# New prices in the clock model that sets a hybrid kernel's issue order: TensorE's spacings and the port of VectorE and GpSimd

## The chip, the core and the metric

The kernel runs on one core of a Trainium2 chip. Five engines take part: TensorE (PE, with its weight loads as PEld), VectorE (DVE), ScalarE (ACT), GpSimd (POOL) and SyncE (SP), which issues the transfers. The metric is the device time of one execution in microseconds (us). Before the change it is 1357.74 us, the median of three runs.

## What is computed

The reference is a backbone of two layers over 1024 latent tokens and a prefix of 256 context tokens, 1024 columns wide, all in float32. Cut to what matters, one layer is:

```python
shift, scale, gate = split(silu(c) @ w_mod + b_mod, 3)            # the context has its own
h = rms_norm(x) * (1 + scale) + shift
p = h @ w_in                                                     # one projection for all branches
a = silu(layer_norm(depthwise_conv31(p.a_val * sigmoid(p.a_glu)))) * silu(p.a_gate)
b = windowed_attention(rope(p.b_q), rope(p.b_k), p.b_v,          # 8 heads, 2 kv heads, +-128 tokens,
                       context keys and values, sink) * silu(p.b_gate)   # and all of the context
g = gla(p.c_q, p.c_k, p.c_v, decay(p.c_lr), chunk=64)            # forwards plus backwards, 4 heads
x = x + gate * (concat(a, b, norm(g) * silu(p.c_gate)) @ w_out)
```

At the end the latent tokens get a last RMSNorm. In the backward and the forward GLA each chunk of 64 tokens adds `(k * exp(b_last - b)).T @ v` to a state that decays from chunk to chunk; `b` is the running sum of the logarithms of the decay.

## The kernel before

The whole problem stays in SBUF as far as it can. Token tiles have 128 rows: two of context (0 and 1) and eight latent ones (2 to 9). Every large product is done in three float32r passes (`three`, L670): high part by high part, high by low and low by high, on weights that `piece` (L615) loads by DMA and splits into two parts (`split`, L362: a copy on ACT or DVE and a subtraction on DVE or POOL). Outputs of 256 or 512 columns accumulate in PSUM banks. A layer runs in two phases. `phase_a` (L1568) makes the projections, the convolution, the GLA and the attention's operands; `phase_bc` (L1627) runs attention and the out-projection side by side.

The pieces of the work that the change touches through the order:

- `conv_taps` (L921): 62 operations on DVE a layer (31 taps by two halves of the channels), `scalar_tensor_tensor` of 1295 columns in layer 0 and 1024 in layer 1, both inputs in SBUF. One is put in whenever DVE has no more than 300 ns of work in the model.
- `rope` (L883), called by `ev_qk_b` (L895) for each pair of token tiles: for each tile of the pair four `tensor_tensor` on POOL (a product with the sine, one with the cosine, a subtraction, an addition), eight a pair. The columns are 128 for the keys and 256 for the queries.
- `gla_states` (L1056), once for each direction `d` (forwards 0, backwards 1) and each of three chunks of columns `c` (256 context tokens, 512 and 512 latent ones): DVE subtracts (`last - b`), ACT takes the exponential, POOL multiplies by the keys in `mix`, PE transposes the product 128 columns at a time (`idr`), ACT copies the result from PSUM, PE makes the state products with the values in four column groups (outputs 32x128), and DVE adds them up chunk by chunk (`scalar_tensor_tensor` on 128x64).
- `u_run` (L1300), `u_head` (L1356), `u_ev` (L1375) and `u_pv` (L1384): a unit of attention is one block of 128 queries and one kv head. PE makes the scores of four heads, DVE the mask and the minimum, ACT the exponential with its sum, then the probabilities are scaled on DVE, POOL or ACT (`scale`, L383). PE transposes them, key tile by key tile and for four heads at a time, ACT and DVE write the high and the low part of each transposed tile (`H`), and PE multiplies them by the values (PV).
- `out_tiles` and `out_mm` (L1465, L1442): the out-projection, at low priority, which fills PE's time between attention's steps.

The order is not written out by hand. Every piece of work is a generator, a lane; what it yields is the condition for its next stage. `loop` (L201) keeps a clock `now`, which is PE's clock in the model, and issues among the stages whose conditions hold by then the one of the highest priority; if there is none, it goes on to the earliest. The conditions are times out of `Model`: `issue` (L117) starts each instruction when its engine and its operands are free, adds the price that `cost` (L94) gives, and notes on the parts of the tiles when they were written and read. `pick` (L356) chooses the engine for work that several can do: the one that would end first by these clocks. `Model` only decides order and engine. What has to wait for what on the chip is up to the semaphores, so a price that is off gives an order that suits the chip less, and nothing else: each engine takes its instructions strictly in the order of issue. Every instruction is issued through `Engine` (L35), so that the profile shows L43 for all of them (L44 after the change).

The model knows one more thing of PE: after an idle time of over 3 us it doubles the prices for 3.8 us (`cold`). It knew nothing of DVE and POOL hindering each other.

Of the kernel before, what the change touches and what calls it, by code (L numbers as in the profile page):

```python
# [34 lines left out]
class Engine:  # L35
    """an engine whose instructions are also put on the model's clock"""
# [12 lines left out]
class Model:  # L49
    """Estimate of when each engine is free and when each part of a tile was last written and read.  # L50
    It only decides the order in which instructions are issued; what has to wait for what is up to Tile."""

    def __init__(self, nc):
        self.nc = nc
        self.clock = dict(pe=0.0, act=0.0, dve=0.0, pool=0.0, sp=0.0, ring=0.0, dma=0.0)
        self.mem, self.memo = {}, {}
        self.end = self.cold = 0.0
        for n, a in (("pe", "tensor"), ("act", "scalar"), ("dve", "vector"), ("pool", "gpsimd"), ("sp", "sync")):
            setattr(self, a, Engine(self, n, getattr(nc, a)))

    def part(self, ap):
        """the times of ap's tile (written, read, written as seen by PE) and the pieces of it that ap covers"""
# [31 lines left out]
    def cost(self, e, op, out, ins, accum=0):  # L94
        n = out.free_size()
        if e == "pe":
            n = ins[-1].free_size()
            p = out.partition_size()
            if ins[0].dtype == F32R:
                return 55.0 if op == "transpose" else max(n / 2.4, 0.84 * p)  # L100
            return (1 if op == "transpose" else 2) * max(n / 1.2, 0.84 * p)
# [13 lines left out]
        return 110 + 1.1 * n  # L115

    def issue(self, e, op, a, k):  # L117
# [19 lines left out]
        else:  # L137
            x = self.cost(e, op, out, ins, len(outs) - 1)
            if e == "pe":
                if "tile_position" in k:  # L140
                    x = x * out.partition_size() / 128.0 + 29
# [15 lines left out]
class Lane:  # L157
    """a generator of stages: what it yields says when its next stage may be issued"""
# [6 lines left out]
class Hybrid:  # L165
# [10 lines left out]
    # ---------------------------------------------------------------- issue order  # L176
# [6 lines left out]
    def when(self, c, lane):  # L183
        """the time from which condition c holds, None if that is not known yet"""
# [16 lines left out]
    def loop(self, last):  # L201
        """issues stages until lane `last` is done: of those that may start by now, the first by priority"""
# [33 lines left out]
    # ---------------------------------------------------------------- memory  # L236
    def memory(self):
# [13 lines left out]
        # a PSUM tile is used by one engine at a time, so there is one a bank, but for two of two banks  # L251
# [18 lines left out]
    def choice(self, cls, wide):  # L270
        """the free slots; those for wide tiles are left to these while self.rsv"""
# [18 lines left out]
    def mix_new(self, dt):  # L290
        """the upper half of mix anew, to hold what it doesn't hold yet"""
# [6 lines left out]
    def mix(self, a, t, p=slice(None)):  # L298
        """tokens t of mix a, or of several that lie in the same half of mix"""
# [6 lines left out]
    def bank_of(self, cls, pair):  # L306
        """the bank that class cls would get"""
# [35 lines left out]
    def at(self, ap):  # L343
        """condition: all that has been issued has written ap"""
        return lambda: self.nc.written(ap)

    def rest(self, ap):
        """condition: nothing issued uses ap any more"""
        return lambda: self.nc.touched(ap)

    def sm_spare(self, cols):
        """like sm(), from the spare place if that is free"""
        return self.get("SF")[:, 0:cols] if self.slots["SF"] else self.sm(cols)

    # engines that can do the same work: the one that is done first
    def pick(self, *opts):  # L356
        """opts: (engine, estimated cost, function)"""
# [4 lines left out]
    def split(self, hi, lo, src):  # L362
        """hi + lo = src exactly, both float32r; src in SBUF"""
# [6 lines left out]
    def copy(self, o, a):  # L370
        """from PSUM"""
# [11 lines left out]
    def scale(self, o, a, s, f=1.0):  # L383
        """o = a * s * f; s one value a partition"""
# [6 lines left out]
    def square(self, junk, a, o):  # L391
        """o = sum of a * a"""
# [6 lines left out]
    # ---------------------------------------------------------------- set-up  # L399
# [37 lines left out]
    def rope_free(self):  # L437
        """between its uses the memory of the rotary table is one more small tile"""
# [3 lines left out]
    def rope_load(self):  # L442
        """generator: the rotary table again"""
# [24 lines left out]
    # ---------------------------------------------------------------- modulation  # L468
    def mod_add(self, l, b0, mt):
        """blocks b0 .. of the modulation from PSUM [128, blocks, 2], with their bias"""  # L470
# [9 lines left out]
    def mod_group(self, l, b0, n, raw):  # L480
        """generator: n blocks of 128 columns of the modulation, four k-tiles at a time in the column groups of the PE array;
        raw: the k-tiles of w_mod, loaded here if None"""
# [32 lines left out]
    # ---------------------------------------------------------------- h  # L515
    def hslot(self, i):
        """chunk and column offset of token tile i in the T-layout h"""
# [6 lines left out]
    def views(self):  # L524
        """the memory of h, free for it once the first weights have gone through"""
# [14 lines left out]
    def rstd(self, ss, scale, n):  # L540
        """(ss * scale + eps) ** -0.5 on [128, n]"""
# [13 lines left out]
    def part_h(self, l, i, k0, n, x):  # L555
        """generator: k-tiles k0 .. k0 + n - 1 of h for token tile i, from its normalised [128, 128 n] piece x"""
# [36 lines left out]
    def first_x(self, i, xt):  # L593
        """generator: token tile i of the input, loaded to xt and normalised there"""
# [16 lines left out]
    # ---------------------------------------------------------------- weights  # L611
# [14 lines left out]
    def load_w(self, key, src, ap, tile=None):  # L626
        """256 weight columns, split into hi and lo; ap(hl, k): k-tiles k and k + 1"""
# [22 lines left out]
    def loader(self):  # L650
        """generator: all weights in the order of their use"""
# [17 lines left out]
    # ---------------------------------------------------------------- in-projection  # L669
    def three(self, out, st, mv, k0, k1):  # L670
        """out += st(hi,lo)^T mv(hi,lo) over k-tiles k0 .. k1 - 1 of 8, three float32r passes"""
# [1159 lines left out]
```

## Time and profile before

| | |
|---|---|
| median of three runs | 1357.74 us (1356.18, 1357.74, 1364.62) |
| span of the profiled execution | 1357.4 us, 24183 instructions |
| mean granted clock of PE | 0.983 |
| busiest engines | PE 1268.0, PEld 1084.6, DVE 951.0, ACT 558.6, POOL 543.8 us |
| idle of PE, 0 to 200 us (loads, modulation, first projections) | 21.6 us |
| idle of PE, 1300 to 1357 us (tail of the out-projection) | 8.7 us |

The profiled execution is one run; its span is compared with sums made from its own rows, and the median with other medians. A row of the profile has the operation, output and inputs by the program's tile names, partitions by elements, type and count. The names: `ps` is a PSUM bank, `WS` split weights, `WR` raw weights and temporaries, `H` and `HC` the split activations and, later, attention's operands, `SM` small tiles, `mix` the branch outputs and the convolution's accumulators, `U` the convolution's input, `idr` the identity matrix. In brackets behind a row of the timeline stands how long the engine had been idle and who released it. A float32 matmul counts as two in the count of a row. "Clock" is the TensorE clock that was granted, 1.0 being full speed.

### The profile page before, as it was taken

What the parts mean: (1) busy time and instruction counts of PE and PEld (TensorE: products, weight loads), DVE (VectorE), ACT (ScalarE), POOL (GpSimd) and SP (SyncE); (2) the same over time, 40 slices, a digit from 0 to 9 for tenths busy, and PEclk for the clock granted to TensorE, in tenths of its full rate; (3) what the DMA queues carried; (4) which work ended last, traced back from release to release, by engine and by line L of the source; (5) the groups of instructions that cost most, each with busy time, mean ns of one, the idle gap of its engine ahead of it and who ended that gap; (6) DMA issues with size and microseconds to landing.
All of it is one profiled execution on the core that took longest, in us unless ns stands there. A gap on an engine that the chain in (4) does not pass through costs nothing.

```text
span 1357.4 us, 24183 instructions
## 1 busy us (share of the span) xinstructions
PE 1268.0 (93%) x9070; PEld 1084.6 (80%) x9070; DVE 951.0 (70%) x1852; ACT 558.6 (41%) x1239; POOL 543.8 (40%) x769
## 2 busy tenths in 40 slices
PE   6999986898999999999999989988899999999997
PEld 3667976787788676887998978977797888898997
DVE  5844895789655366875666686896957478887864
ACT  3720351121223364665663451251113156776751
POOL 1410046766222233464353032046783244645530
PEclk9999997899999999999999999989999999999999
DMA  9353112321212433343113452113322113311112
GB/s 331 137 147 97 55 32 58 83 79 44 67 32 65 131 118 89 104 129 97 42 55 98 132 191 62 55 37 78 97 57 77 34 48 101 98 44 51 62 37 78
DMA packets 105045, 116.46 MB, mean 86 GB/s; under 512 B 38464, under 2 KB 65376, under 8 KB 104928
## 3 DMA queue, kind: packets, MB, share of 16 engines
q1 hardware_dynamic: 104928, 114.92, 28.4%
q8 instruction: 71, 1.16, 0.3%
q14 instruction: 46, 0.38, 0.1%
HBM read 95.47 MB, written 19.42 MB: 85 GB/s over the span
## 4 chain that ended last, share of the span: by engine, by line
PE 49%; DVE 10%; POOL 8%; issue 5%; DMA 4%; ACT 2%; SPq 0%; POOLq 0%; DVEq 0%; ACTq 0%
PE ps L43 49%; DVE SM L43 5%; POOL SM L43 5%; DVE H L43 2%; DMA WR<-in_w_in_dram 2%; POOL WR L43 2%; DVE WS L43 1%; DVE mix L43 1%; ACT SM L43 1%; POOL tir L43 1%; DMA SM<-kd 0%; DMA SM<-x 0%; SPq L43 0%; DMA WR<-in_w_out_dram 0%; DMA x<-SM 0%
## 5 line engine op out<-in xcount | busy, mean ns | idle before, releaser
L43 PE MATMUL ps<-H,WS 128*128 128x512 f32 x1344 | 339.2, 400 | 4.2 <-DVE stat L43 2.4
L43 PEld LDWEIGHTS ps<-H,WS 128*128 128x128 f32 x1344 | 245.6, 189 | 71.4 <-issue 17.6
L43 ACT ACTIVATE SM<-ps 128x512 f32<-128x512 f32 (+4 forms) x172 | 91.0, 533 | 427.0 <-PE ps L43 353.5
L43 PE MATMUL ps<-WS,H 128*128 128x256 f32 x1704 | 254.0, 291 | 6.3 <-DVE SM L43 3.7
L43 PEld LDWEIGHTS ps<-WS,H 128*128 128x128 f32 x1704 | 229.2, 195 | 21.9 <-issue 11.6
L43 PE MATMUL ps<-idr,SM 128*128 128x128 f32 (+1 forms) x1076 | 150.1, 272 | 34.6 <-POOL SM L43 27.8
L43 DVE SCALAR_TENSOR_TENSOR mix<-U,small,mix 128x1295 f32<-128x1295 f32 (+1 forms) x120 | 176.6, 1517 | 0.2
L43 PEld LDWEIGHTS ps<-idr,SM 128*128 128x128 f32 (+1 forms) x1076 | 122.8, 142 | 58.3 <-POOL SM L43 32.9
L43 DVE SCALAR_TENSOR_TENSOR H<-ps,H 128x512 fp32r<-128x512 f32 x160 | 106.2, 683 | 59.7 <-ACT H L43 59.6
L43 POOL TENSOR_TENSOR SM<-SM,SM 128x256 f32<-128x256 f32 (+4 forms) x89 | 70.5, 799 | 179.8 <-ACT SM L43 142.6
L43 ACT ACTIVATE H<-ps 128x512 fp32r<-128x512 f32 x176 | 99.6, 597 | 86.7 <-PE ps L43 81.6
L43 POOL TENSOR_TENSOR tir<-tir,mhalf 128x1 f32<-128x1 f32 (+2 forms) x55 | 44.4, 810 | 205.3 <-DVE tir L43 177.8
L43 ACT ACTIVATE SM<-SM,stat 128x641 f32<-128x641 f32 (+2 forms) x144 | 110.4, 768 | 34.9 <-DVE stat L43 27.1
L43 DVE CUSTOM_DVE_ANT_0 SM<-ps,SM,small 128x640 f32<-128x640 f32 (+2 forms) x128 | 101.9, 808 | 18.8 <-PE ps L43 18.5
L43 PE MATMUL ps<-H 128*128 128x512 f32 x320 | 99.3, 412 | 2.0 <-DVE H L43 1.8
L43 PE MATMUL ps<-H,H 128*128 128x256 f32 x552 | 98.2, 286 | 0.0
L43 POOL TENSOR_TENSOR SM<-SM,WR 128x128 f32<-128x128 f32 (+2 forms) x113 | 88.5, 801 | 13.1 <-DVE SM L43 9.3
L43 PE MATMUL ps<-SM,SM 128*32 128x128 f32 (+4 forms) x764 | 80.3, 291 | 13.4 <-DVE SM L43 8.8
L43 POOL TENSOR_SCALAR SM<-SM,tir 128x640 f32<-128x640 f32 (+2 forms) x86 | 73.5, 869 | 38.5 <-DVE tir L43 30.4
L43 PEld LDWEIGHTS ps<-H,H 128*128 128x128 f32 x552 | 82.3, 189 | 4.7 <-issue 3.4
L43 PE MATMUL ps<-WS,SM 128*128 128x256 f32 x248 | 69.4, 280 | 0.0
L43 PE MATMUL ps<-H,SM 128*128 128x256 f32 x248 | 69.4, 280 | 0.0
(150 smaller groups left out, 2126.7 us busy)
## 6 DMA issues: line engine op xcount, KB each, us to landing
WR<-in_w_in_dram SPq DMA_DIRECT2D x80, 256.0 KB, 3.9
WR<-in_w_mod_dram SPq DMA_DIRECT2D x64, 256.0 KB, 3.0
WR<-in_w_out_dram SPq DMA_DIRECT2D x32, 256.0 KB, 3.3
SM<-vd SPq DMA_DIRECT2D x116, 64.0 KB, 2.4
x<-SM SPq DMA_DIRECT2D x20, 256.0 KB, 2.5
SM<-x SPq DMA_DIRECT2D x20, 256.0 KB, 4.6
qd<-SM SPq DMA_DIRECT2D x18, 256.0 KB, 2.2
mix<-in_x_dram SPq DMA_DIRECT2D x8, 512.0 KB, 8.0
```

The lines of the kernel that those rows point to most:

```text
L43: r = getattr(self._e, op)(*a, **k)
```

## The change

No instruction of the computation is changed. Three prices of the model are, and the order and the choice of engines follow from them:

1. `cost`, for PE. A float32r matmul of n columns costs max(64, n / 2.4 + 14) ns instead of max(n / 2.4, 0.84 p) with p output partitions; a float32r transpose max(64, n / 2.4) instead of 55. A float32 matmul costs 2 max(58, n / 1.2 + 5) instead of 2 max(n / 1.2, 0.84 p), and a float32 transpose 109 instead of max(n / 1.2, 0.84 p).
2. `issue`, for matmuls in column groups (`tile_position`): the price scaled by the partitions plus 29 ns gets a lower bound, half the full price for more than 64 columns and the full price otherwise.
3. `shared`, new. The model keeps the last 64 intervals of DVE instructions that have two SBUF inputs, or are a `tensor_copy` or `tensor_scalar` wholly in SBUF, and of POOL instructions that read SBUF. An instruction of that kind whose start falls into an interval of the other engine starts at its end. Its own price stays the same. The prices of ACT, DVE and POOL, the lanes, their priorities and all conditions stay the same too.

Comments and docstrings are removed besides, which shifts line numbers by one or more.

```diff
@@ class Model: __init__
         self.mem, self.memo = {}, {}
+        self.port = dict(dve=deque(maxlen=64), pool=deque(maxlen=64))
         self.end = self.cold = 0.0
@@ cost
             n = ins[-1].free_size()
-            p = out.partition_size()
             if ins[0].dtype == F32R:
-                return 55.0 if op == "transpose" else max(n / 2.4, 0.84 * p)
-            return (1 if op == "transpose" else 2) * max(n / 1.2, 0.84 * p)
+                return max(64.0, n / 2.4 + (0 if op == "transpose" else 14))
+            return 109.0 if op == "transpose" else 2 * max(58.0, n / 1.2 + 5)
@@ new
+    def shared(self, e, op, out, ins, t, x):
+        sb = [i.free_size() > 1 for i in ins if "PSUM" not in str(i.space).upper()]
+        if e == "dve":
+            both = sum(sb) > 1
+            fast = op in ("tensor_copy", "tensor_scalar") and sum(sb) and len(sb) == len(ins) and "PSUM" not in str(out.space).upper()
+            if not (both or fast):
+                return t
+        elif not sb:
+            return t
+        for a, b in self.port["pool" if e == "dve" else "dve"]:
+            if a <= t < b:
+                t = b
+                break
+        self.port[e].append((t, t + x))
+        return t
@@ issue
             x = self.cost(e, op, out, ins, len(outs) - 1)
+            if e in self.port:
+                t = self.shared(e, op, out, ins, t, x)
             if e == "pe":
                 if "tile_position" in k:
-                    x = x * out.partition_size() / 128.0 + 29
+                    x = max(x * out.partition_size() / 128.0 + 29, 0.5 * x if ins[-1].free_size() > 64 else x)
```

What the program issues by engine, before and after (PE and SP are the same): DVE 1698 and 1642, ACT 1036 and 1062, POOL 763 and 793.

The new order differs from the old in many places. Three are shown, each as it stood and as it stands.

The first is POOL's order in layer 0, at the second chunk of the GLA states. `SM_262` is the forward direction's exponential and `SM_264` the backward one's, multiplied by the keys in `mix`; `SM_267` is a pair of key tiles of attention with its temporary `WR_268`. Before:

```order
L43 TENSOR_TENSOR WR_268_1771<-SM_267_1770,SM_1_65 128x128
L43 TENSOR_TENSOR SM_267_1770<-SM_267_1770,SM_1_65 128x128
L43 TENSOR_TENSOR SM_267_1770<-SM_267_1770,WR_268_1771 128x2x32 x2
...
L43 TENSOR_TENSOR SM_267_1770<-SM_267_1770,WR_268_1771 128x2x32 x2
L43 TENSOR_TENSOR SM_262_1734<-SM_262_1734,mix 128x512
L43 TENSOR_TENSOR SM_264_1742<-SM_264_1742,mix 128x512
```

Now:

```order
L44 TENSOR_TENSOR SM_262_1725<-SM_262_1725,mix 128x512
L44 TENSOR_TENSOR WR_268_1776<-SM_267_1775,SM_1_65 128x128
L44 TENSOR_TENSOR SM_267_1775<-SM_267_1775,SM_1_65 128x128
L44 TENSOR_TENSOR SM_267_1775<-SM_267_1775,WR_268_1776 128x2x32 x2
...
L44 TENSOR_TENSOR SM_267_1775<-SM_267_1775,WR_268_1776 128x2x32 x2
L44 TENSOR_TENSOR SM_264_1733<-SM_264_1733,mix 128x512
```

The forward product moved ahead of the pair's eight rotary operations; the backward one still stands behind all eight. On DVE ten taps stood between the subtraction of the backward direction and the next state sums, and now six.

The second is PE's order at the same place: the projections' matmuls (`WS` by `H`), the transposes of the two products (`idr`) and the state products (32x128). Before:

```order
L43 MATMUL ps_67<-WS_189_1014,H_6_111 128x256 x24
L43 MATMUL ps_66<-WS_189_1014,H_0_104_491 128x256 x12
...
L43 MATMUL ps_67<-WS_189_1014,H_0_104_491 128x256 x12
L43 MATMUL ps_70<-idr,SM_262_1734 128x128 x4
L43 MATMUL ps_67<-WS_189_1014,H_1_105_492 128x256 x12
L43 MATMUL ps_71<-idr,SM_264_1742 128x128 x4
L43 MATMUL ps_68<-SM_183_1004,SM_263_1735 32x128 x4
```

Now:

```order
L44 MATMUL ps_67<-WS_190_1034,H_6_111 128x256 x36
L44 MATMUL ps_66<-WS_190_1034,H_0_103_503 128x256 x12
L44 MATMUL ps_70<-idr,SM_262_1725 128x128 x4
L44 MATMUL ps_66<-WS_190_1034,H_1_104_504 128x256 x12
L44 MATMUL ps_71<-SM_184_1013,SM_263_1726 32x128 x4
L44 MATMUL ps_66<-WS_190_1034,H_0_103_503 128x256 x12
L44 MATMUL ps_71<-SM_185_1014,SM_263_1726 32x128 x4
L44 MATMUL ps_66<-WS_190_1034,H_1_104_504 128x256 x12
L44 MATMUL ps_68<-idr,SM_264_1733 128x128 x4
```

Ahead of the forward transposes stood 84 matmuls of 256 columns, now 48; 12 stood between the forward and the backward transposes, now 36 and two groups of state products.

The third is PE's order in one unit of attention in layer 1 (block 6, first kv head): the end of the transposes of its first three key tiles, the out-projection's matmuls behind them, and the first PV matmuls (128x512). Before:

```order
L43 MATMUL ps_68<-idr,SM_1698_12442 128x128
L43 MATMUL ps_68<-idr,SM_1699_12443 128x128
L43 MATMUL ps_71<-H_0_104_491,H_6_111 128x256 x2
L43 MATMUL ps_71<-H_0_104_491,SM_1715_12553 128x256
...
L43 MATMUL ps_69<-H_1_105_492,SM_1716_12554 128x256
L43 MATMUL ps_70<-H_6_111 128x512 x6
```

Now:

```order
L44 MATMUL ps_71<-idr,SM_1689_12433 128x128
L44 MATMUL ps_71<-idr,SM_1690_12434 128x128
L44 MATMUL ps_70<-WS_1465_10975,H_6_111 128x256 x2
L44 MATMUL ps_70<-WS_1465_10975,SM_1711_12555 128x256
...
L44 MATMUL ps_70<-WS_1465_10975,SM_1711_12555 128x256
L44 MATMUL ps_69<-H_6_111 128x512 x2
```

Between the transposes and the PV matmuls stood 44 rows of the out-projection, now eight (12 matmuls), and the PV matmuls of one key tile come by themselves.

More of the change, by code (lines that the diff above doesn't have):

```diff
@@ L1 @@
+from collections import deque
 from contextlib import ExitStack
```

## The prediction

> **What bounds the kernel now.** I read the page first: busy shares, then the chain that ended last. The chain is followed back from the last instruction.
>
> ```profile
> PE 1268.0 (93%) x9070; PEld 1084.6 (80%) x9070; DVE 951.0 (70%) x1852; ACT 558.6 (41%) x1239; POOL 543.8 (40%) x769
> PE 49%; DVE 10%; POOL 8%; issue 5%; DMA 4%; ACT 2%; SPq 0%; POOLq 0%; DVEq 0%; ACTq 0%
> ```
>
> TensorE (PE) works 1268.0 of the 1357.4 us of the profiled execution's span and is half of the last chain. No matmul is added or taken away, so an issue order can gain only from the 89.4 us in which PE does nothing and from stretches at a lower clock. The execution lies 0.3 us under the median of 1357.74, so sums made against 1357.4 stand for the median as well. About 1% is what a measurement of this kernel can tell from no change: 13.6 us, that is, 1344 to 1371.
>
> The second view is the table by stages (us from the start; PE, PEld, DVE, ACT, POOL busy, then the granted clock, the DMA share and GB/s):
>
> ```profile
> 200.00:300.00 100.00, 83.04 (x763) 75.56 (x762) 70.91 (x102) 17.27 (x45) 67.23 (x75) 0.90 0.28 75
> 300.00:800.00 500.00, 480.37 (x3380) 403.70 (x3379) 331.31 (x735) 231.38 (x523) 188.88 (x297) 0.99 0.31 93
> 800.00:1000.00 200.00, 186.32 (x1388) 166.44 (x1388) 162.96 (x228) 57.04 (x117) 88.25 (x104) 0.97 0.24 66
> 1000.00:1300.00 300.00, 291.58 (x2082) 255.89 (x2081) 219.51 (x474) 157.16 (x351) 147.86 (x229) 1.00 0.22 64
> ```
>
> The weak stage is 200 to 300, the GLA states of layer 0: 17 us idle and a clock of 0.90. Attention and out-projection (300 to 800 and 1000 to 1300) are 96 and 97% full; there PE has nearly everything that an order can give it, and can lose some. The waits of PE (total, times, longest):
>
> ```profile
> PE ps L43 <- POOL SM L43: 28.6, 15, 10.1
> PE ps L43 <- DVE SM L43: 15.7, 17, 2.5
> ```
>
> GpSimd (POOL) is the largest cause, with one wait of 10.1 us. The timeline around it (start, us, what, count, idle before it and its releaser):
>
> ```profile
> 202.73 7.12 PE L43 MATMUL ps<-WS,H 128*128 128x256 f32 x58
> 202.82 15.93 DVE L43 SCALAR_TENSOR_TENSOR mix<-U,small,mix 128x1295 f32<-128x1295 f32 x10
> 204.66 1.52 POOL L43 TENSOR_TENSOR WR<-SM,SM 128x128 f32<-128x128 f32 x1 [4.06 <-ACT SM L43]
> 206.26 1.60 POOL L43 TENSOR_TENSOR SM<-SM,SM 128x128 f32<-128x128 f32 x1
> 207.94 3.01 POOL L43 TENSOR_TENSOR SM<-SM,WR 128x64 f32<-128x64 f32 x2
> 210.91 1.72 POOL L43 TENSOR_TENSOR WR<-SM,SM 128x128 f32<-128x128 f32 x1
> 212.71 1.60 POOL L43 TENSOR_TENSOR SM<-SM,SM 128x128 f32<-128x128 f32 x1
> 214.38 3.00 POOL L43 TENSOR_TENSOR SM<-SM,WR 128x64 f32<-128x64 f32 x2
> 217.35 3.75 POOL L43 TENSOR_TENSOR SM<-SM,mix 128x512 f32<-128x512 f32 x2
> 219.93 1.11 PE L43 MATMUL ps<-idr,SM 128*128 128x128 f32 x4 [10.08 <-POOL SM L43]
> 221.07 0.45 POOL L43 TENSOR_TENSOR WR<-SM,SM 128x128 f32<-128x128 f32 x1
> 221.60 0.46 POOL L43 TENSOR_TENSOR SM<-SM,SM 128x128 f32<-128x128 f32 x1
> ```
>
> Eight rotary operations of a key tile stand on POOL ahead of the two decay products (128x512) that the GLA transposes need. Each takes 1.5 to 1.7 us while DVE runs convolution taps (ten in 15.93 us, 1.59 each), and 0.45 us once the taps are over: one POOL operation gets through per tap. The old model holds 150 + 2.1 x 128 = 419 ns for such an operation, wherever it stands; the product then looked ready some 8 us too early.
>
> [...]
>
> The clock adds to this wait (windows of PE: busy, granted clock, DMA share, GB/s), and two more places behind POOL look alike:
>
> ```profile
> 220.00:225.00 5.00, 5.00 (x29) 0.50 0.17 38
> 225.00:230.00 5.00, 5.00 (x47) 0.93 0.32 73
> 256.00:263.00 7.00, 5.06 (x32) 0.53 0.28 77
> 257.94 1.11 PE L43 MATMUL ps<-idr,SM 128*128 128x128 f32 x4 [4.68 <-POOL SM L43]
> 905.74 0.69 PE L43 MATMUL ps<-idr,SM 128*128 128x128 f32 x2 [3.26 <-POOL SM L43]
> 927.51 0.66 PE L43 MATMUL ps<-idr,SM 128*128 128x128 f32 x4 [3.31 <-POOL SM L43]
> ```
>
> After the 10.08 us wait PE works 5 us at half clock and 5 at 0.93: 2.5 + 0.35 = 2.85 us lost. After the 4.68 us wait it works 5.06 us at 0.53: 2.4 lost. Together 5.2.
>
> **The change part by part.** It removes and adds no instruction of the program; it changes three prices by which the next stage and the engine are chosen.
>
> *TensorE's prices.* Two spacings from the trace tell whether they fit: 58 matmuls of 256 columns in 7.12 us above, 0.123 each, and six of 512 here from 1293.82 to 1295.20, 0.230 each:
>
> ```profile
> 1284.74 1.47 PE L43 MATMUL ps<-idr,SM 128*128 128x128 f32 x12
> 1285.97 0.48 PE L43 MATMUL ps<-H,H 128*128 128x256 f32 x2
> ...
> 1293.82 1.54 PE L43 MATMUL ps<-H 128*128 128x512 f32 x6
> 1295.20 1.03 PE L43 MATMUL ps<-idr,SM 128*128 128x128 f32 x8
> ```
>
> The old formula gives 107.5 and 213 ns, the new 121 and 227. So the model's PE clock was 7 to 12% fast, and the new one is right. By itself that costs and gains nothing; it acts through the order. A slower PE clock makes ACT, DVE and POOL, whose prices stay, look relatively quicker, so the scheduler puts less PE work between a result and its use.
>
> *The port, second chunk of the GLA states (the order's first two places).* The forward product moves ahead of the eight rotary operations; the backward one stays behind the same eight. When does it come? The rotary operations start at 204.66 as before, since the copy that releases them stays where it is. Ahead of the backward chain only 6 taps now stand in DVE's row instead of 10: they last from 202.82 to about 202.8 + 6 x 1.6 = 212.4. Until then five of the eight get through; the rest take 3 x 0.5, the product 1.3 (two take 3.75 above, the first of them beside the last tap): 212.4 + 1.5 + 1.3 = 215.2. PE had nothing left at 202.73 + 7.12 = 209.85. By the new order it has the same matmuls of 256 columns up to the backward transposes, and the forward transposes and two groups of state matmuls besides, each like this row:
>
> ```profile
> 232.50 0.43 PE L43 MATMUL ps<-SM,SM 128*32 128x128 f32 x8
> ```
>
> 209.85 + 3 x 0.43 = 211.1, so it waits 4.1 us instead of 10.1: **-6.0**. Bounds: 0 if the whole wait only changes direction; -10.1 if POOL is through in time.
>
> *Third chunk.* The 4.68 us were for the backward product, behind the eight rotary operations of a query pair. Now both products stand together behind a key pair's eight, and the forward one, with three taps beside it, comes some 2 to 4 us after PE by the same sum; I take 3.0: **-1.7** (0 to -4.7). In layer 1 the backward product still stands behind eight rotary operations, so the 3.26 and 3.31 stay: 0 (bound -6.6).
>
> *The clock.* A wait of 4.1 us will still be followed by a slow stretch; 3.26 us was followed by one too (905.74), as the row of 800 to 1000 with its 0.97 fits. I give half of the third chunk's 2.4 us: **-1.3** (0 to -5.2).
>
> [...]
>
> *Work that changes engine.* The order counts 56 instructions fewer on DVE, 26 more on ACT, 30 more on POOL: weight pieces, score scaling, modulation.
>
> ```profile
> L43 DVE CAST WS<-WR 128x512 fp32r<-128x512 f32 x52 | 28.2, 544 | 43.3 <-DMA WR<-in_w_in_dram 34.6 <-PE ps L43 8.6
> L43 POOL TENSOR_SCALAR SM<-SM,tir 128x640 f32<-128x640 f32 x53 | 51.0, 977 | 14.6 <-DVE tir L43 12.4 <-DMA WR<-in_w_out_dram 1.1 <-PE ps L43 0.8
> ```
>
> At 0.54 us apiece DVE sheds 30 us, ACT gains some 16 (0.6 each), POOL 24 (0.8, under the scaling's 0.98). Weighted by the chain's 10, 2 and 8%: -3.0 + 0.3 + 1.9 = **-0.8**. All else of it is covered by PE, which is busy; if PE's cover went, DVE's 30 us would be the gain and POOL's 24 the price.
>
> *Thinner covers.* In the GLA outputs of layer 0 two waits behind DVE tiles have less PE work ahead of them; at the mean of such a wait, 15.7 / 17 = 0.9: **+2** (0 to +4). In attention the place is the order's third: a unit of layer 1, block 6. These are the rows that make its probabilities usable by PE after their transposes:
>
> ```profile
> 1285.88 1.58 ACT L43 ACTIVATE H<-ps 128x512 fp32r<-128x512 f32 x3
> 1287.51 1.86 DVE L43 SCALAR_TENSOR_TENSOR H<-ps,H 128x512 fp32r<-128x512 f32 x3
> ```
>
> The transposes begin at 1284.74; the first tile is ready at 1287.51 + 0.62 = 1288.1, 3.4 us later. Before, 44 rows of matmuls covered that to 1293.82. Now 12 matmuls stand there: 12 transposes (1.23) + 12 x 0.12 = 2.7 us, then the first PV matmul, so 0.7 us of wait. Over all 36 units (two kv heads, ten blocks in layer 0 and eight in layer 1), counting the order and multiplying by spacings, the median cover goes from 3.3 to 3.2 us and the lowest tenth from 2.3 to 2.2: four or five units lose about 0.7: **+3** (0 to +25, if all 36 lose 0.7).
>
> Sum: 1357.4 - 6.0 - 1.7 - 1.3 - 0.8 + 2 + 3 = 1352.6. **Predicted: 1353 us**; the start, the boundary of the layers and the tail have nearly the same order, and I leave 0 for them.
>
> **The rivals.** *Faster: POOL's waits go.* If taps hold POOL up less than one operation each, because the sixth tap ends the contention earlier or POOL's last operations slip between, all of PE's waits behind POOL can go (28.6), with the clock's 5.2, at best 1323.6; with a few us left, **1328**. For it: the six taps, and the shed DVE work. Against: layer 1's two places and the backward product are not moved out from behind the rotary operations.
>
> *The wait only moves.* The backward product, which stays behind the same eight rotary operations and reads a later result of DVE, is as late as the forward one was, and PE has only 1.3 us more ahead of it. Then nothing is left but the small terms: 1357.4 + 2 + 3 - 0.8 - 3 = **1359**, no change. Against it: four taps fewer in the way. The change would then do on DVE and POOL what it says, and not on PE.
>
> *Slower: attention's covers.* With PE priced 12% higher and ACT, DVE and POOL as low as before (POOL's scaling of 640 columns measures 977 ns against the model's 110 + 1.1 x 640 = 814, ACT's copy of a tile 1.58 / 3 = 0.53 us against 512 / 1.2 + 50 = 477 ns), every unit is scheduled as if its chain were shorter than it is. It decides once most units have a chain of 3.4 us and a cover of 2.7 or less: 36 x 0.7 = 25, so 1352.6 - 3 + 25 = **1375**. For it: PE there is 96 to 97% busy and has no slack to give, and the unit above. Against: the median cover hardly falls.
>
> **How the numbers follow.** The forecast, 1345 to 1359 on its own, has 0.42; faster 0.24; the wait that only moves 0.14; slower 0.20. About a fifth of the forecast's own cases lie under 1344 (both chunks' waits gone, attention free): faster by over 1% is 0.24 + 0.09 = 0.33. Within 1%: the rest of the forecast, 0.33, and the moved wait: 0.47. Slower: 0.20. The range reaches to the faster rival's 1328 and to the slower one's 1375, and leaves a tenth outside on either side: 1328 to 1376.
>
> **What would show it.** In the new profile: a wait of 3 to 6 us behind POOL between 205 and 225 in place of 10.1, with a slow stretch still after it; PE's waits behind POOL 18 to 23 us in total; the two 3.3 us waits near 905 and 928 still there; DVE at 915 to 925 us busy, POOL at 560 to 570; PE's waits behind DVE and ACT tiles up by 3 to 6. The forecast is wrong if 200 to 300 keeps its 17 idle us (then the wait moved), if the stages of attention lose more than 10 us of PE time (then the slower rival), or if the waits behind POOL fall under 10 us.

## The result: the changed kernel is slower by 0.7%

The changed kernel takes 1369.32 us, the median of five runs (1366.39 to 1369.88), the kernel before 1357.74 (1356.18 to 1364.62). The ratio is 1.0069 with a 95% interval of 1.0048 to 1.0089. The profiled execution spans 1368.1 us, 10.7 more than that of before. The time lies within the range of the prediction and on the other side of no change: 1353 was forecast. In what follows, times are medians of all executions, ratios go by the undisturbed ones alone, and the profiled execution of `nudge_before` was a disturbed one, so that kernel has no row in the tables of lost time.

The page of the changed kernel, and PE's waits (total, times, longest):

```profile
PE 1273.6 (93%) x9070; PEld 1088.1 (80%) x9070; DVE 942.5 (69%) x1797; ACT 574.9 (42%) x1264; POOL 551.2 (40%) x799
```

```profile
PE ps L44 <- POOL SM L44: 23.6, 15, 5.1
PE ps L44 <- ACT SM L44: 13.3, 8, 7.2
PE ps L44 <- DMA HC<-in_w_mod_dram: 13.1, 3, 12.3
PE ps L44 <- DVE SM L44: 12.9, 15, 2.5
```

The engines moved as the order said: ACT rose by 16 us and the waits behind POOL fell from 28.6 to 23.6. DVE fell by 8.5 us only. The waits behind ACT doubled (from 6.0), with one of 7.2 us where the longest had been 2.8. By stages (PE, PEld, DVE, ACT, POOL busy, clock, DMA share, GB/s):

```profile
200.00:300.00 100.00, 83.88 (x769) 74.39 (x770) 77.69 (x118) 16.90 (x44) 64.44 (x78) 0.95 0.29 75
300.00:800.00 500.00, 478.41 (x3390) 401.02 (x3389) 313.20 (x689) 237.60 (x536) 195.33 (x307) 0.99 0.30 92
800.00:1000.00 200.00, 186.61 (x1371) 166.32 (x1371) 158.63 (x224) 61.06 (x127) 81.99 (x106) 0.96 0.25 67
1000.00:1300.00 300.00, 287.65 (x2012) 252.44 (x2011) 217.88 (x452) 157.82 (x343) 151.15 (x230) 0.98 0.20 61
```

Between 200 and 300 the clock rose from 0.90 to 0.95. Between 1000 and 1300 PE did 2012 instructions where it had done 2082, at a clock of 0.98 instead of 1.00: there most of the time was lost on balance.

Windows of fixed times compare different work. So I set each matmul's start against the work before it: every record of PE in order, priced at the spacing of its form (0.227 us for 512 float32r columns, 0.121 for 256, 0.109 for a float32 transpose, and so on; 1206 us in every kernel here; at a granted clock of 1.00 the medians from start to start in the trace of the kernel before are 0.228, 0.120 and 0.109). Start less work done is the time lost so far. Cut at 170, 320, 670, 795, 1020 and 1170 us of work, it gives for each profiled execution what was lost in each piece. In the kernel before, these cuts lie at 203, 385, 765, 897, 1149 and 1312 us: the start with the first chunk of the GLA states, the rest of the GLA of layer 0, its attention and out-projection, the boundary with layer 1's first projections, its GLA and the beginning of its attention, the rest of its attention, the tail.

```
                 start  GLA 0  att 0  bound  GLA 1  att 1   tail |  lost
before            32.7   32.2   30.5    6.6   27.0   12.6    1.0 | 142.7
after             36.2   25.6   31.1   11.5   27.9   21.6   -0.3 | 153.7
```

The GLA stage of layer 0 gained 6.6 us. The start lost 3.5, the boundary 4.9, layer 1's attention 9.0.

Over the whole kernel the loss is idle time and slow clock in about equal parts. PE's idle time (span less busy time) rose from 89.4 to 94.5 us. The busy time that fell into stretches at half clock (granted 0.50), taken by half, rose from 14.9 to 20.7; that half is an estimate, since at 0.50 matmuls of 256 columns stood 0.213 us apart, by the median in both traces, against 0.120 at 1.00. Layer 1's attention, the largest loss, shows the same: between its cuts, 1149 to 1312 and 1152.3 to 1324.3, PE was idle for 5.9 us and is now for 10.0; and where the clock never fell before, two stretches now run at half of it. They hold 9.34 us of work, so 4.7 us are lost (PE busy, clock, DMA share, GB/s; before, then now):

```profile
1149.00:1312.00 163.00, 157.14 (x1175) 1.00 0.20 61
```

```profile
1152.30:1324.30 172.00, 161.97 (x1166) 0.97 0.17 54
1187.20:1194.00 6.80, 5.94 (x26) 0.50 0.26 79
1293.00:1296.40 3.40, 3.40 (x17) 0.50 0.03 7
```

The place that the prediction worked out, in the changed kernel's timeline:

```profile
203.80 1.29 POOL L44 TENSOR_TENSOR SM<-SM,mix 128x512 f32<-128x512 f32 x1 [3.49 <-ACT SM L44]
205.57 9.71 DVE L44 SCALAR_TENSOR_TENSOR mix<-U,small,mix 128x1295 f32<-128x1295 f32 x6
...
212.19 1.72 POOL L44 TENSOR_TENSOR WR<-SM,SM 128x128 f32<-128x128 f32 x1
213.99 1.60 POOL L44 TENSOR_TENSOR SM<-SM,SM 128x128 f32<-128x128 f32 x1
215.66 0.59 POOL L44 TENSOR_TENSOR SM<-SM,WR 128x64 f32<-128x64 f32 x2
216.22 1.26 POOL L44 TENSOR_TENSOR SM<-SM,mix 128x512 f32<-128x512 f32 x1
217.53 0.92 PE L44 MATMUL ps<-idr,SM 128*128 128x128 f32 x4 [4.15 <-POOL SM L44]
```

The forward product runs at 203.80 and the forward transposes wait for nothing. The backward product comes after six taps and the eight rotary operations, and PE waits 4.15 us for it where 4.1 was forecast. Both ends of that sum came 2.3 us later than in it, since the whole place moved with the loss at the start: the product ended at 217.5 instead of 215.2, and PE had nothing left at 213.4 instead of 211.1.

### The profile page after: what moved, and what is told of

Its sections match the earlier page's. It is cut to its first block, busy times and chain, and to the rows that moved or that the text cites. A ratio compares the mean times of both kernels' runs of the same rounds, so it can differ in the third digit from the quotient of the medians.

```text
span 1368.1 us, 24225 instructions
## 1 busy us (share of the span) xinstructions
PE 1273.6 (93%) x9070; PEld 1088.1 (80%) x9070; DVE 942.5 (69%) x1797; ACT 574.9 (42%) x1264; POOL 551.2 (40%) x799
## 5 line engine op out<-in xcount | busy, mean ns | idle before, releaser
L44 PE MATMUL ps<-WS,H 128*128 128x256 f32 x1704 | 259.6, 295 | 2.9 <-DVE H L44 1.3
L44 PEld LDWEIGHTS ps<-WS,H 128*128 128x128 f32 x1704 | 233.6, 199 | 13.5 <-issue 8.2
L44 POOL TENSOR_TENSOR SM<-SM,SM 128x256 f32<-128x256 f32 (+4 forms) x89 | 66.9, 760 | 136.2 <-ACT SM L44 103.8
L44 PE MATMUL ps<-H 128*128 128x512 f32 x320 | 96.2, 408 | 0.1
L44 POOL TENSOR_TENSOR SM<-SM,WR 128x128 f32<-128x128 f32 (+2 forms) x115 | 80.7, 718 | 28.2 <-DVE SM L44 10.0
L44 DVE TENSOR_TENSOR SM<-SM,mix 32x128 f32<-32x128 f32 x144 | 67.7, 470 | 3.5 <-ACT SM L44 1.4
```

Source lines behind the costliest of these rows:

```text
L44: r = getattr(self._e, op)(*a, **k)
```

## The experiments

Three theories stood at first. Theory 1: TensorE's higher prices thin the covers in attention. Theory 2: `shared`, the model's port, does the harm. Theory 3: every change of a price deals the whole order anew, and the kernel before is a good hand.

**Half of the change each.** `pe_only` leaves out the call of `shared`; `port_only` keeps it and has TensorE's old prices.

```diff
-            if e in self.port:
-                t = self.shared(e, op, out, ins, t, x)
```

> The changed kernel without the port: TensorE's new prices (column groups too), no shared intervals. Theory 1, TensorE's prices thin the covers: the slower TensorE clock in the model puts less matmul work between a result and its use, so attention loses most of what the changed kernel lost there (some 14 us over both layers) and the GLA stage of layer 0 keeps its old 10 us wait; 1368 to 1376. Theory 2, the port does the harm (it turns work away from VectorE and late orders follow): within 4 us of before, 1354 to 1362. Theory 3, luck of the order: anywhere within 12 us of before, with the losses at other places than in the changed kernel.

> The kernel before with the shared intervals of VectorE and GpSimd alone, TensorE's old prices. Theory 1: the wait behind GpSimd in the GLA states of layer 0 shrinks as in the changed kernel (10.1 to 4 or 5 us) and attention loses nothing: 1349 to 1355. Theory 2: as slow as the changed kernel, 1366 to 1372. Theory 3: anywhere within 12 us of before.

Measured: 1374.52 us, ratio 1.0108 (1.0085 to 1.0132), and 1385.34 us, 1.0198 (1.0162 to 1.0233). Each half is slower than the whole. `pe_only` lies within theory 1's range, but the wait behind POOL that theory 1 kept at 10 us was 5.69 there; `port_only` lies outside all three ranges.

**A price moved by about 1% or less.** `nudge_after`, `nudge_after2` and `nudge_after3` have 13, 15 and 14.5 in place of 14; the four `nudge_before` have 0.845, 0.835, 0.85 and 0.8425 in place of 0.84.

```diff
-                return max(64.0, n / 2.4 + (0 if op == "transpose" else 14))
+                return max(64.0, n / 2.4 + (0 if op == "transpose" else 13))
```

```diff
-                return 55.0 if op == "transpose" else max(n / 2.4, 0.84 * p)
+                return 55.0 if op == "transpose" else max(n / 2.4, 0.845 * p)
```

> The changed kernel with 13 ns instead of 14 behind the n / 2.4 of a float32r matmul: one price off by 1 per cent, far less than the change itself moved it. Theories 1 and 2: the same causes act, so within 3 us of the changed kernel, 1366 to 1372. Theory 3: a small nudge moves the time as much as the whole change did, 5 us or more either way.

> The changed kernel with 15 ns instead of 14 behind n / 2.4. Theory 3: 1365 to 1385, that is, the changed kernel is an ordinary draw. Theories 1 and 2: 1366 to 1372.

> The changed kernel with 14.5 ns instead of 14. If the changed kernel is an ordinary draw of its prices: 1362 to 1385.

> The kernel before with 0.845 instead of 0.84 in the price of a float32r matmul, which makes those of 256 columns 0.6 per cent dearer (107.5 to 108.2 ns) and leaves those of 512 as they are. Theories 1 and 2: within 3 us of before, 1355 to 1361. Theory 3: 5 us or more either way, with waits at places where neither kernel has them.

> The kernel before with 0.835 instead of 0.84 in the price of a float32r matmul (256 columns at 106.9 ns instead of 107.5). Luck of the order (theory 3): the kernel before is one draw among many and a good one, so this is slower by 8 to 25 us, with the loss mostly in layer 1's attention. Theories 1 and 2: within 3 us of before.

> The kernel before with 0.85 instead of 0.84 (256 columns at 108.8 ns instead of 107.5). Luck of the order: slower than before by 5 to 25 us, like the two nudges ahead of it. If the kernel before is an ordinary draw: within 3 us of it.

> The kernel before with 0.8425 instead of 0.84 (256 columns at 107.8 ns instead of 107.5). If the kernel before is a rare good draw: 1365 to 1395, with 19 us or more of TensorE's time lost in layer 1's attention where before loses 9. If it is an ordinary one: about as often below 1358 as above.

Measured, in that order: 1381.04 (1.0148, 1.0121 to 1.0175), 1369.74 (1.0085, 1.0057 to 1.0113), 1383.23 (1.0170, 1.0135 to 1.0204); 1377.94 (1.0138, 1.0106 to 1.0171), 1367.59 (1.0047, 1.0023 to 1.0070), 1395.14 (1.0274, 1.0231 to 1.0317), 1395.37 (1.0259, 1.0231 to 1.0287). What they lost, piece by piece, with the two halves:

```
                 start  GLA 0  att 0  bound  GLA 1  att 1   tail |  lost
pe_only           38.4   23.9   33.8   12.2   30.1   20.5   -0.7 | 158.2
port_only         40.3   22.7   49.6    4.6   27.3   25.8   -0.4 | 169.9
nudge_after       32.0   24.8   38.0    5.4   35.7   24.2   -0.2 | 160.0
nudge_after2      34.2   22.8   36.0   12.3   31.1   18.8   -0.6 | 154.6
nudge_after3      34.4   27.5   42.5   11.9   28.7   19.9   -0.3 | 164.6
nudge_before2     35.6   31.2   26.6    7.6   33.0   20.7   -0.5 | 154.2
nudge_before3     31.3   33.2   41.8   12.6   27.2   34.1   -0.5 | 179.8
nudge_before4     35.3   35.5   40.8    7.0   30.8   28.1    2.3 | 179.8
```

Two things follow. First, theories 1 and 2 fall. `nudge_before`, a nudge of 0.6%, costs 1.4%, twice the whole change, and `nudge_before2`, which makes PE's matmuls cheaper, loses in layer 1's attention nearly as much as the changed kernel does. With TensorE's old prices `port_only` loses more there than `pe_only`. No cause with a fixed sign does that. In every one of these orders layer 1's attention costs 18.8 to 34.1 us, and in the kernel before 12.6: there PE is idle for 8.9 us or more in each of them and at least one stretch runs at half clock, against 5.9 us and none. Of eleven orders timed, the kernel before is the fastest, by 0.5%; `nudge_before2`, the changed kernel and `nudge_after2` come next, with intervals that overlap. Theory 3 has the kind of the result and not its size: the two halves, `nudge_before3` and `nudge_before4` are slower than its ranges allowed, and `nudge_before2` lost a little less than its 8 us. `nudge_after2` fits all three theories and tells nothing by itself.

Second, the part of the change that was aimed at does its work. In GLA 0 the five orders with TensorE's new prices lose 22.8 to 27.5 us and `port_only` 22.7; the four with the old prices lose 31.2 to 35.5. In start and GLA 0 together, where part of this goes again, the five lose 57 to 62 us (changed kernel 61.8, the nudges 56.8, 57.0 and 61.9, `pe_only` 62.3) and `port_only` 63.0; the four with the old prices lose 64.5 to 70.8. The gain is not owed to `shared` alone: `pe_only` has it too. Over the whole kernel the neighbours of the old prices have a mean ratio of 1.018 (four), those of the new ones 1.013 (three), with wide overlap.

**Only the products ahead, all other orders kept.** `overtake_before` keeps the order of before on PE, DVE, ACT and SP. The model books as before, but rotary operations are put on POOL late, behind decay products that stand directly behind them. `overtake_after` does the same to the changed kernel.

```diff
+            if self._n == "pool" and m.hold is True:
+                m.late.append(lambda: getattr(self._e, op)(*a, **k))
+                return m.issue(self._n, op, a, k)
+            if self._n in ("pool", "sp") and not m.first:
+                m.flush()
```

> The kernel before with its own prices and its own order on TensorE, VectorE, ScalarE and SyncE; only where GLA decay products stand directly behind a tile pair's rotary operations on GpSimd, the products go first (the clock model still books them in the old order). This tells the place of the change's gain apart from all the rest of its reordering. Theory A, the waits behind the rotary operations are real cost: the 10.1 and 4.7 us waits in layer 0 and the 3.3 us one near 928 go, with some 5 us of half clock; 1335 to 1345. Theory B, the wait comes back at the next thing that is late (values, state sums, or the rotary operations' own readers): 1352 to 1358.

> The changed kernel with the same rule, products ahead of the rotary operations they stand directly behind. Theory A: the backward product's 4.3 us wait in layer 0 and two of layer 1's go: 1356 to 1363, which leaves it above the kernel before with the same rule by what the changed kernel loses in attention. Theory B: 1366 to 1370.

Measured: 1361.71 us, ratio 1.0035 (1.0011 to 1.0059), and 1373.45, 1.0112 (1.0094 to 1.0129). Theory B: nothing is gained; both came out 3 to 4 us above its ranges. In `overtake_before` the products are done at 201.5 and 204.7, and PE waits at the same place as long as before, for another reason:

```profile
203.40 1.29 POOL L49 TENSOR_TENSOR SM<-SM,mix 128x512 f32<-128x512 f32 x1 [1.92 <-ACT SM L49]
...
214.58 3.00 POOL L45 TENSOR_TENSOR SM<-SM,WR 128x64 f32<-128x64 f32 x2
217.61 0.38 SPq L49 DMA_DIRECT2D kd<-SM  x1
218.09 6.25 SPq L49 DMA_DIRECT2D SM<-vd  x8
219.86 1.57 ACT L49 ACTIVATE SM<-ps 128x512 f32<-128x512 f32 x3 [16.54 <-DMA kd<-SM]
...
221.16 0.66 PE L49 MATMUL ps<-SM,SM 128*32 128x128 f32 x8 [10.82 <-DMA SM<-vd]
```

SyncE (SPq) took these issues in order: the store of the rotary outputs (`kd`) stands there ahead of the loads of the GLA values (`vd`), it waits until the rotary operations end at 217.6, and the loads come behind it, from 218.09 on. ACT's copies, the row that waited 16.54 us, hang on the same store. The kernel before has the same store on SP, hidden behind the wait for POOL; in the changed kernel four of the loads have moved ahead of it:

```profile
200.63 17.17 SPq L43 DMA_DIRECT2D kd<-SM  x2
217.89 10.99 SPq L43 DMA_DIRECT2D SM<-vd  x10
```

```profile
200.82 2.49 SPq L44 DMA_DIRECT2D SM<-vd  x4
216.28 0.38 SPq L44 DMA_DIRECT2D kd<-SM  x1
```

**The stores off SyncE's queue.** `pool_store` issues them from POOL, right behind the operations; `both_before` and `both_after` have this and the products ahead.

```diff
-            nc.sync.dma_start(dst[i0:i0 + 2].rearrange("s p c -> p s c"), s3)
+            to = dst[i0:i0 + 2].rearrange("s p c -> p s c")
+            nc.issue("sp", "dma_start", (to, s3), {})
+            nc.gpsimd._e.dma_start(to, s3)
```

> The kernel before, its order kept on every engine; only the stores of the rotary outputs (kd, qd) are issued from GpSimd's queue, right behind the operations that make them, instead of from SyncE's queue, where the loads of the GLA values stand behind them. The theory of two waits in parallel: TensorE still waits some 10 us at 210 for the decay product behind the rotary operations, since that alone is enough; the value loads now come early; 1354 to 1360. If the value loads alone were what counted: 1335 to 1345. What issuing a store costs on GpSimd is not known from any run; if it is 1 us apiece, 1360 or more.

> Both edits at once on the kernel before: the decay products ahead of the rotary operations, and the stores off SyncE's queue. TensorE's, VectorE's and ScalarE's orders are unchanged. Theory of two waits in parallel: now nothing holds the state products at 210 and 253 (10.1 and 4.7 us), nor the 3.3 us one near 928, and the half clock behind them goes: 1335 to 1345. If a third thing is late there (the copies of the transposes, the state sums behind the taps): 1350 to 1358.

> The same two edits on the changed kernel. Two waits in parallel: its 4.3 us wait at 213, those of 1.9 and 2.0 at 234 to 239 and part of layer 1's go, 1353 to 1362; it stays above the kernel before with both edits by the 10 us that it lost in attention.

Measured: 1374.38 us (1.0114, 1.0078 to 1.0151), 1378.02 (1.0154, 1.0117 to 1.0190), 1384.26 (1.0198, 1.0168 to 1.0229). `pool_store` came out in its last case, 1360 or more; the other two lie 20 us or more above every range given for them. In `pool_store` the wait behind POOL is still 8.84 us, as the theory of two waits had it. With both waits gone a third one holds the same place in `both_before`, as long as the first:

```profile
225.24 1.57 ACT L49 ACTIVATE SM<-ps 128x512 f32<-128x512 f32 x3 [17.39 <-DMA kd<-SM]
226.37 0.65 PE L49 MATMUL ps<-SM,SM 128*32 128x128 f32 x8 [11.85 <-ACT SM L49]
```

ACT, in order as well, stands 17.39 us at the copy of the next pair of key tiles, which waits until the rotary pair is stored (`<-DMA kd<-SM`); the copies of the GLA transposes are behind it. So three in-order queues, POOL, SP and ACT, hang on the same rotary pair, and with one or two of them out of the way the wait at this place was still 8.8 to 11.9 us. The store from POOL itself costs about 0.75 us on POOL and lands later (below), and these kernels lose in layer 1 too: GLA 1 lost 36.9 and 36.2 us instead of 27.0. By which waits the stores do that was not followed. That the third wait gone too would free the place was not tried by itself.

**The rotary pair made shorter.** `rope4_before` does the embedding of a tile pair in four operations of twice the size instead of eight, while the model books the eight, so that the other engines' orders stay; `rope4_after` is the same edit on the changed kernel.

```diff
+        e.tensor_tensor(g(tmp), g(x), sin, op=ALU.mult)
+        e.tensor_tensor(g(x), g(x), cos, op=ALU.mult)
+        e.tensor_tensor(h(x)[:, :, :, 0], h(x)[:, :, :, 0], h(tmp)[:, :, :, 1], op=ALU.subtract)
+        e.tensor_tensor(h(x)[:, :, :, 1], h(x)[:, :, :, 1], h(tmp)[:, :, :, 0], op=ALU.add)
```

> The kernel before with the rotary embedding of a tile pair in four GpSimd operations of twice the size instead of eight; the clock model still books eight, so the order on TensorE, VectorE, ScalarE and SyncE is that of before. Theory of one turn per tap: the rotary block beside taps takes 4 x 1.6 = 6.5 us instead of 13, all that hangs on it comes 6 us earlier; the 10.1 us wait shrinks to 3 or 4, the 4.7 and 3.3 us waits to under 1, half clock goes in part: 1337 to 1347. If the contention goes by the amount of data and not by the number of operations: 1354 to 1360.

> The changed kernel with the same four rotary operations a pair, its order kept on the other engines. One turn per tap: the 4.3 us wait at 213 and the ones at 905 and 927 shrink: 1354 to 1362, still some 12 us above the kernel before with the same edit, since its attention is not touched. By the amount of data: 1366 to 1372.

Measured: 1348.72 us, ratio 0.9913 (0.9891 to 0.9935), faster than both kernels, though 2 us above what was expected (of the smaller waits 4.68 became 0.35 and 3.31 became 1.81, but 3.26 stayed at 3.23); and 1370.61, 1.0073 (1.0050 to 1.0095), no gain over the changed kernel. The place in `rope4_before`:

```profile
201.04 19.46 DVE L43 SCALAR_TENSOR_TENSOR mix<-U,small,mix 128x1295 f32<-128x1295 f32 x10
...
201.35 1.85 POOL L901 TENSOR_TENSOR WR<-SM,SM 128x256 f32<-128x256 f32 x1 [4.89 <-ACT SM L43]
203.28 1.89 POOL L902 TENSOR_TENSOR SM<-SM,SM 128x256 f32<-128x256 f32 x1
205.25 1.60 POOL L903 TENSOR_TENSOR SM<-SM,WR 128x128 f32<-128x128 f32 x1
206.82 1.71 POOL L904 TENSOR_TENSOR SM<-SM,WR 128x128 f32<-128x128 f32 x1
208.49 5.04 POOL L43 TENSOR_TENSOR SM<-SM,mix 128x512 f32<-128x512 f32 x2
...
211.07 1.11 PE L43 MATMUL ps<-idr,SM 128*128 128x128 f32 x4 [3.37 <-POOL SM L43]
```

An operation of 256 columns takes 1.85 or 1.89 us beside the taps and one of 128 columns 1.60 or 1.71, where 128 columns took 1.5 to 1.7 and 64 columns 1.5: one turn per tap in these rows, at either size. The block takes 7.2 us instead of 12.7, and the wait 3.37 instead of 10.08. The gain stays in the end, because nothing else was dealt anew:

```
                 start  GLA 0  att 0  bound  GLA 1  att 1   tail |  lost
overtake_before   30.9   32.7   31.9    6.4   28.6   13.4    1.0 | 145.0
pool_store        32.8   35.8   31.0    5.8   36.9   15.0    1.0 | 158.4
both_before       35.1   37.5   33.7    5.3   36.2   13.4    1.0 | 162.2
rope4_before      30.6   26.2   30.4    6.8   23.4   13.5    1.0 | 131.9
rope4_after       33.9   27.5   30.9   12.0   29.1   22.8   -0.3 | 155.9
```

In the four kernels with the order of before, layer 1's attention loses 13.4 to 15.0 us, near its 12.6, and none of the others comes near that. In the changed kernel the shorter rotary pair saves 2.3 us at the start and nothing in the GLA stage, where other waits have become the longest; its prediction of 1354 to 1362 missed.

## Why the prediction was wrong

The forecast of the place held, and the forecast for the rest of the kernel failed. Two steps failed: the 0 for the start, the boundary of the layers and the tail, which measured +7.1 us together (3.5 + 4.9 - 1.3), and the +3 for thinner covers in attention, which measured +9.6. The forecast was 4.8 us less, and the lost time rose by 11.0; these two steps make 13.7 of the 15.8 us between.

- *TensorE's prices fit:* right as a reading of the spacings; that a right price by itself costs nothing, and acts through the order alone, was right too, but the size of that action was not asked.
- *Second chunk, -6.0:* right, 4.15 us of wait for 4.1. *Third chunk, -1.7:* it has two waits now, 1.73 for the forward product and 1.80 for the values, 3.5 in place of 4.68: -1.2. *The clock, -1.3, and the two waits in the GLA outputs, +2:* with the chunks this made -7.0 for the stage; 32.2 to 25.6 is -6.6 (the clock measured -2.1, the waits in the GLA outputs +3.2). The two 3.3 us waits of layer 1, put at 0, became 5.11 and 2.91. The reason given for the 10.08 us was too simple. That wait had three causes side by side, and taking away only the one named in the profile gave nothing (`overtake_before`). The changed order also set value loads ahead of the store on SP and had fewer taps in the way; that it gained by these is read from the rows above, and no run tests them alone.
- *Work that changes engine, -0.8:* ACT's +16 came, POOL rose by 7 instead of 24, and DVE lost 8.5 instead of 30; what that did to the time no run shows apart. Part of DVE's saving went into dearer operations elsewhere: its small products in the GLA outputs took 470 ns a piece instead of 419.

```profile
L43 DVE TENSOR_TENSOR SM<-SM,mix 32x128 f32<-32x128 f32 x144 | 60.4, 419 | 5.2 <-ACT SM L43 3.1
```

```profile
L44 DVE TENSOR_TENSOR SM<-SM,mix 32x128 f32<-32x128 f32 x144 | 67.7, 470 | 3.5 <-ACT SM L44 1.4
```

- *Thinner covers in attention, +3:* mis-sized. Layer 0 lost 0.6 more, layer 1 9.0, of which about half is clock; the term counted waits alone. At the unit shown in the prediction the waits stand elsewhere than I put them, ahead of the transposes, where the scalings on ACT and POOL are late, and half clock follows from 1293.0 on:

```profile
1291.05 0.33 PE L44 MATMUL ps<-idr,SM 128*128 128x128 f32 x1 [1.63 <-ACT SM L44]
...
1291.76 1.04 POOL L44 TENSOR_SCALAR SM<-SM,tir 128x640 f32<-128x640 f32 x1
...
1292.85 2.52 PE L44 MATMUL ps<-idr,SM 128*128 128x128 f32 x11 [1.48 <-POOL SM L44]
```

- *"The start, the boundary of the layers and the tail have nearly the same order, and I leave 0 for them":* of the two steps that failed, the one with no reason but the likeness of the orders. The start lost 3.5 us, mostly at the first chunk's product. DVE's subtraction for it came at 192.40 instead of 190.15, and PE's wait grew from 2.03 to 3.59 us. The clock was 1.00 behind the first wait; behind the second it was 0.50 for 6.8 us, which costs 2.8. Before, then now:

```profile
192.05 0.44 PE L43 MATMUL ps<-idr,SM 128*128 128x128 f32 x2 [2.03 <-POOL SM L43]
```

```profile
194.30 0.69 PE L44 MATMUL ps<-idr,SM 128*128 128x128 f32 x2 [3.59 <-POOL SM L44]
193.90:200.70 6.80, 5.61 (x40) 0.50 0.48 116
```

The boundary lost 4.9. In both kernels ACT's scaling of the next layer's input stands behind two weight pieces that wait for their loads; but PE now comes to its transposes at 784.6 instead of 787.5 us, and the scaling begins 1.5 us later, at 791.06 instead of 789.53, behind a second piece whose load came 1.7 us later. Ahead of the boundary the changed kernel had lost 2.5 us less than the kernel before, behind it 2.4 us more. Before and after:

```profile
781.83 5.63 PE L43 MATMUL ps<-H,WS 128*128 128x512 f32 x24
...
788.67 0.63 ACT L43 ACTIVATE WS<-WR 128x512 fp32r<-128x512 f32 x1 [0.30 <-DMA WR<-in_w_in_dram]
789.53 1.39 ACT L43 ACTIVATE SM<-SM,tir 128x512 f32<-128x512 f32 x2 [0.22 <-DMA SM<-x]
...
790.30 1.32 PE L43 MATMUL ps<-idr,SM 128*128 128x128 f32 x8 [2.85 <-ACT SM L43]
```

```profile
780.36 4.25 PE L44 MATMUL ps<-H,WS 128*128 128x512 f32 x18
...
790.34 0.63 ACT L44 ACTIVATE WS<-WR 128x512 fp32r<-128x512 f32 x1 [1.95 <-DMA WR<-in_w_in_dram]
...
791.06 1.42 ACT L44 ACTIVATE SM<-SM,tir 128x512 f32<-128x512 f32 x2
...
791.84 3.42 PE L44 MATMUL ps<-idr,SM 128*128 128x128 f32 x16 [7.23 <-ACT SM L44]
```

- *The rivals.* The one that ends slower named the place, attention, and was the nearest in sign; its mechanism, covers thinner because the model's PE clock runs slower, does not explain `port_only`, which has the old prices, or `nudge_before2`, which has lower ones: both lose there as well. No rival said what happened: that the kernel before holds an order that is better than those its own prices give nearby, so that each of the ten changes of prices tried first cost what that order was worth.

Why the order of before is so good in layer 1's attention stays open. The runs show that it is rare and what it is worth (less idle time and no half clock), not how it came about. If the old price had been chosen by timing kernels, its neighbours would be slower by that choice alone; nothing here tells.

## What to carry to other kernels

Where a list scheduler deals the order, a change of its prices is a new hand for the whole kernel: time a few neighbours of the old and of the new setting, 1% apart, before a difference of 1% is put down to the change. A wait in the profile names the cause that ended last; look in every in-order queue for what else hangs on the same producer, since removing the named cause may move nothing (10.08 us of wait in the kernel before, 10.82 at the same place in `overtake_before`). In the kernel before, the edit that made the shared producer shorter and left PE's order alone gained 0.9%; in the changed kernel the same edit gained nothing, so such a gain too is one of a given order.

## What the hardware showed

- Beside the taps, POOL got one operation per tap in the rows of the kernel before and of `rope4_before`, of 128 or of 256 columns alike: 1.5 to 1.7 and 1.85 to 1.89 us there, against 0.45 for 128 columns and 0.73 for 256 alone. The taps paid for the larger ones: ten took 15.93 us beside the small operations and 19.46 beside the large ones, where both products of 512 columns fell among the taps too.
- Half clock (granted 0.50) came behind several short waits as well as behind one long one, as the 10.08 us in the kernel before (0.50 from 220 to 225 us). Ahead of the stretch from 1293.0 on, the changed kernel's PE waited 1.63 and 1.48 us, with 0.33 us of work between; at the one from 1187.2 on, no single wait was over 1.29 us.
- A store issued from POOL kept it for 0.73 to 0.94 us in `pool_store` (195 to 250 us), and landed later than one from SP in the kernel before (median from issue to landing 3.6 us against 2.2 for `qd`, 256 KB each):

```profile
qd<-SM POOLq DMA_DIRECT2D x18, 256.0 KB, 3.6
```

```profile
qd<-SM SPq DMA_DIRECT2D x18, 256.0 KB, 2.2
```
